# Four blocks of a feed-forward product as a two-by-two scheme of seven products, with its operands kept in HBM

## The chip, the cores and the metric

The kernel runs on one core of one Trainium2 chip. The metric is the device time of one execution in microseconds (us), as the median of several runs. A core has five engines that run beside each other: TensorE (PE; its weight loads are listed as PEld), VectorE (DVE), ScalarE (ACT), GpSimd (POOL) and SyncE (SP), on whose queue this kernel issues all of its DMAs.

## The reference

One decoder layer on 1024 tokens of width 1024: a half-step feed-forward part, a token mixer with two groups of heads, and a second feed-forward part, each followed by a layer norm.

```
x = LN1(ALPHA * x + 0.5 * swiglu(x, w_gate1, w_up1, w_down1))
x = LN2(ALPHA * x + mixer(x))
x = LN3(ALPHA * x + 0.5 * swiglu(x, w_gate2, w_up2, w_down2))
swiglu(x, g, u, d) = (silu(x @ g) * (x @ u)) @ d        # D_FF = 2816
```

All of it is in float32. Only the two swiglu parts matter here.

## The kernel before

**Tiles.** The 2816 hidden channels are 22 blocks of 128. Tokens are two halves of 512. For a block and a half, the hidden value silu(gate) * up is a tile of 128 channels by 512 tokens; w_down is applied with a chunk of 128 tokens of it as the stationary operand and a block of w_down, 128 channels by 512 output columns (again two halves), as the moving one. The results are added on DVE into `acc`, eight tiles of 128 tokens by 1024 columns (`down`, L213 to L235).

**Precision.** Each float32 operand is split into a high part (a cast on ACT, L135) and a low part (a subtraction on DVE, L136), and a product is three matmuls: high by high, high by low, low by high.

**Blocks in pairs.** Blocks 2 to 11 of the first feed-forward part and blocks 8 to 17 of the second are worked in pairs by `ffn_pairs` (L580). Gate and up of a pair are a two-by-two block product done with seven products instead of eight (`PRODUCTS`, `weight_sums` L472, `project` L505): each product P1 to P7 is 12 matmuls (four pieces of the sums of tokens by three). The sums of tokens are made once (`token_sums` L452, `last_sums` L462); the sums of weight halves are made for each pair on DVE from four loads (t11, t21, t12, t22) and a fifth tile t2. Products with one target accumulate in one PSUM bank; two banks serve the gate (tag pa) and two others the up product (tag pm). `keep` copies an intermediate value out of the bank on ACT, and `done` finishes one of four hidden tiles, "11" to "22" (token half, block of the pair). There, for the up product, the hidden tile is split at once into its parts gh and gl (L534 to L536).

**w_down of a pair** is done without such a scheme: `down_turns` makes 16 tiles (2 column halves x 2 token halves x 4 chunks), each of 2 blocks x 3 matmuls, in the steps marked d of TURNS, between the products of the next pair; the last pair's 16 steps come at the end. `halves_of` loads and splits the w_down blocks.

**Order and look-ahead.** A turn is one product (12 matmuls) or one d step (6 matmuls). The list `need` holds the weight operands in the order of their use, and the loop at L616 makes them up to DEEP = 4 ahead of the turn. A scheduler then sets the order on each engine by a model of the times, near to the written order but not equal to it; on SP a DMA that waits holds up those behind it.

**Buffers.** Raw loads go to a ring of 7 tiles with the tag wr, split weights to 6 pairs wh and wl, split hidden values to 4 pairs gh and gl, hidden values to 4 tiles gs and kept products to 3 tiles sn. A PSUM bank is 128 x 512 float32; there are 2 with the tag pa, 3 with pd and 3 with pm.

**Around it.** `run` (L1074) begins with blocks 0 and 1 of the first part for both halves, without the scheme for seven products (`hidden_first` L363, `hidden` L351). In this stretch acc holds raw x; `load_acc` loads x into acc again afterwards, beside the first turns, where the token sums are made too.

Of the kernel before, what the change touches and what calls it, by code (L numbers as in the profile page):

```python
# [10 lines left out]
F32 = mybir.dt.float32  # L11
# [37 lines left out]
TURNS = "ggddddgddddgddddgddddgguuuuuuu"  # L49
DEEP = 4  # L50
# [36 lines left out]
class Layer:  # L87
    def __init__(self, tc, ctx, a):
# [13 lines left out]
        self.sx, self.kept = {}, {}  # L102
# [241 lines left out]
    def up(self, w, half, s, pool, tags, bufs):  # L344
        ps = yield from self.proj(w, half)
        self.nc.vector.tensor_tensor(s[:], s[:], ps[:], ALU.mult)
        hs = [self.wt(pool, [HT], t, bufs, F32R) for t in tags]
        self.split(hs[0][:], hs[1][:], s[:])
        return hs
# [155 lines left out]
    def project(self, ops, hid, up):  # L505
# [9 lines left out]
        def done(n, w):  # L515
# [45 lines left out]
    def down_turns(self, ops, hid):  # L561

        for d in range(2):
            for i in range(2):
                for c in range(4):
                    yield
                    hs = [hid[f"{i + 1}1"], hid[f"{i + 1}2"]]
                    ws = [{d: ops[n, d]} for n in range(2)]
                    now(self.down(hs, ws, i, 0.5, [c], cuts=((d * HT, (d + 1) * HT),)))

    def halves_of(self, blocks):
        for d in range(2):
            for b in blocks:
                raw = self.u("wr", self.wp)
                self.nc.sync.dma_start(raw[:], b[:, HALVES[d]])
                hl = [self.wt(self.wp, [HT], "w" + e, BUFS["w"], F32R) for e in "hl"]
                self.split(hl[0][:], hl[1][:], raw[:])
                yield hl

    def ffn_pairs(self, idx, fs, before=None, beside={}):  # L580

        gu, wd = self.a[f"gu{idx}"], self.a[f"wd{idx}"]
        order = [n for n, b in PRODUCTS]
        turns, need = [], []

        def plan(f, before, kinds):

            hid, work, asks = {}, {}, {}  # L590
            if before:
                keys = [(n, d) for d in range(2) for n in range(2)]
                asks["d"] = [keys[:2]] + [[]] * 7 + [keys[2:]] + [[]] * 7
                work["d"] = {}, before[1], self.halves_of([wd[before[0] + n] for n in range(2)])
            if f is not None:
                for up in range(2):

                    blocks = [m[:, sl] for sl in HALVES for m in (gu[f, up], gu[f + 1, up])]
                    asks["gu"[up]] = [[n] for n in order]
                    work["gu"[up]] = {}, hid, self.weight_sums(order[4:], *blocks)  # L600
            makes = {k: self.down_turns(w[0], w[1]) if k == "d" else self.project(w[0], w[1], k == "u") for k, w in work.items()}
            for make in makes.values():
                next(make)
            for kind in kinds:
                if kind in work:
                    ops, _, weights = work[kind]
                    for n in asks[kind].pop(0):
                        need.append((ops, n, weights))
                    turns.append((makes[kind], len(need)))
            return f, hid  # L610

        for f in range(fs.start, fs.stop, 2):
            before = plan(f, before, TURNS)
        plan(None, before, "d" * 16)
        made = 0
        for t, (make, asked) in enumerate(turns):  # L616
            while made < min(asked + DEEP, len(need)):
                ops, n, weights = need[made]
                ops[n] = next(weights)
                made += 1  # L620
            for work in beside.get(t, ()):
                work()
            next(make, None)

# [449 lines left out]
    def run(self):  # L1074
# [5 lines left out]
        with self.phase("fs") as self.fs, self.phase("fa") as self.fx:  # L1080
            self.scr = "gs", self.fx
            hs = [self.hidden_first(self.fx, ("gh", "gl"), 4)]
            hs.append(now(self.hidden(1, 1, (0, 1), self.fx, ("gh", "gl"), 4)))
            hid = {f"{i + 1}{j + 1}": hs[j][i] for i in range(2) for j in range(2)}
            beside = {t: [lambda q=t: self.token_sums(q)] for t in range(KB // 2)}
            for t in range(4):
                beside[t] += [lambda c=c: self.load_acc(c, 0) for c in (2 * t, 2 * t + 1)]
                beside[6 + t] = [lambda c=c: self.load_acc(c, 1) for c in (2 * t, 2 * t + 1)]
                beside[6 + t].append(lambda q=t: self.last_sums(q))
            self.ffn_pairs(1, range(2, K1), (0, hid), beside)  # L1090
# [7 lines left out]
        with self.phase("fs") as self.fs, self.phase("fb") as self.fx:  # L1098
# [4 lines left out]
            self.ffn_pairs(2, range(K2, NF - LAST), beside={t: [lambda q=t: self.last_sums(q)] for t in range(KB // 2)})  # L1103
# [115 lines left out]
```

## Time and profile before

| | |
|---|---|
| time, median of 3 runs | 2053.87 us (2052.97 to 2054.53) |
| time of the profiled execution | 2053.73 us |
| its span, first to last instruction | 2051.8 us |
| mean granted clock of TensorE | 0.997 |
| PE busy | 2020.1 us, 98%, 10052 instructions |
| DVE busy | 1370.5 us, 67%, 2925 instructions |
| ACT busy | 849.3 us, 41%, 1685 instructions |
| DMA | 251.19 MB, mean 122 GB/s |

The profile is of one execution. A group's row names the line, the engine, the operation and its tiles, the count, the time busy and the mean duration in nanoseconds, and the idle time of the engine before these instructions with what ended it. A row of a stretch gives, for each engine, the busy time in that stretch and the number of instructions that began in it. Matmuls are pipelined, so a matmul's drawn duration is longer than the distance between the starts of two; neighbours on DVE overlap a little too. Some matmul records can be missing, a few per cent at most.

### The profile page before, as it was taken

What the parts mean: (1) busy time and instruction counts of PE and PEld (TensorE: products, weight loads), DVE (VectorE), ACT (ScalarE), POOL (GpSimd) and SP (SyncE); (2) the same over time, 40 slices, a digit from 0 to 9 for tenths busy, and PEclk for the clock granted to TensorE, in tenths of its full rate; (3) what the DMA queues carried; (4) which work ended last, traced back from release to release, by engine and by line L of the source; (5) the groups of instructions that cost most, each with busy time, mean ns of one, the idle gap of its engine ahead of it and who ended that gap; (6) DMA issues with size and microseconds to landing.
All of it is one profiled execution on the core that took longest, in us unless ns stands there. A gap on an engine that the chain in (4) does not pass through costs nothing.

```text
span 2051.8 us, 28207 instructions
## 1 busy us (share of the span) xinstructions
PE 2020.1 (98%) x10052; PEld 1650.5 (80%) x10052; DVE 1370.5 (67%) x2925; ACT 849.3 (41%) x1685; POOL 50.2 (2%) x87
## 2 busy tenths in 40 slices
PE   9999999999999999999999999999999999999998
PEld 7788888888888777788788777788788888888887
DVE  5865566545668787746887687667856766556566
ACT  4423333232554444445466545454433423333332
POOL 0000000000000000000100000000000000000000
PEclk9999999999999999999999999999999999999999
DMA  4711112565554344435354434333443311112331
GB/s 172 248 46 58 52 62 86 180 197 188 172 195 143 125 144 144 142 119 182 124 193 132 133 108 123 95 103 114 139 138 119 113 57 47 62 52 88 122 118 63
DMA packets 136653, 251.19 MB, mean 122 GB/s; under 512 B 15552, under 2 KB 16064, under 8 KB 136512
## 3 DMA queue, kind: packets, MB, share of 16 engines
q1 hardware_dynamic: 136512, 249.39, 37.7%
q8 instruction: 79, 1.29, 0.3%
q14 instruction: 62, 0.51, 0.1%
HBM read 206.34 MB, written 42.99 MB: 122 GB/s over the span
## 4 chain that ended last, share of the span: by engine, by line
PE 85%; DVE 8%; ACT 2%; DMA 2%; issue 1%; POOL 0%; SPq 0%; DVEq 0%; ACTq 0%; POOLq 0%
PE pa L207 10%; PE pa L208 10%; PE pa L210 10%; PE pd L229 9%; PE pd L231 9%; PE pd L230 8%; PE pm L547 3%; PE pm L548 3%; PE pm L549 3%; PE pa L547 3%; PE pa L548 3%; PE pa L549 3%; PE pm L1041 1%; DVE wl L136 1%; PE pm L640 1%
## 5 line engine op out<-in xcount | busy, mean ns | idle before, releaser
L135 ACT CAST wh<-wr 128x512 fp32r<-128x512 f32 (+1 forms) x461 | 285.7, 621 | 701.6 <-PE pa L208 207.7
L207 PE MATMUL pa<-xh,wh 128*128 128x512 f32 x1168 | 469.7, 402 | 9.2 <-ACT xh L135 4.6
L136 DVE TENSOR_TENSOR wl<-wr,wh 128x512 fp32r<-128x512 f32 (+1 forms) x461 | 314.6, 686 | 229.5 <-ACT wh L135 226.5
L208 PE MATMUL pa<-xl,wh 128*128 128x512 f32 x1168 | 461.6, 395 | 0.1
L210 PE MATMUL pa<-xh,wl 128*128 128x512 f32 x1152 | 454.3, 395 | 0.0
L234 DVE SCALAR_TENSOR_TENSOR acc<-pd,acc 128x512 f32<-128x512 f32 x433 | 292.9, 685 | 97.3 <-PE pd L231 94.9
L207 PEld LDWEIGHTS pa<-xh,wh 128*128 128x128 f32 x1168 | 220.7, 189 | 56.1 <-ACT xh L135 5.7
L208 PEld LDWEIGHTS pa<-xl,wh 128*128 128x128 f32 x1168 | 220.7, 189 | 42.8 <-DVE xl L136 2.1
L210 PEld LDWEIGHTS pa<-xh,wl 128*128 128x128 f32 x1152 | 217.3, 189 | 43.1
L229 PE MATMUL pd<-wh,gh 128*128 128x512 f32 (+1 forms) x450 | 175.0, 390 | 0.5 <-DVE acc L234 0.4
L231 PE MATMUL pd<-wh,gl 128*128 128x512 f32 (+1 forms) x450 | 174.8, 389 | 0.0
L230 PE MATMUL pd<-wl,gh 128*128 128x512 f32 (+1 forms) x450 | 174.8, 388 | 0.0
L229 PE MATMUL pd<-wh,hh 128*128 128x512 f32 x352 | 141.6, 406 | 1.5 <-ACT xf L278 1.5
L230 PE MATMUL pd<-wl,hh 128*128 128x512 f32 x352 | 139.9, 398 | 1.0 <-DVE wl L136 1.0
L231 PE MATMUL pd<-wh,hl 128*128 128x512 f32 x352 | 139.4, 398 | 0.0
L149 ACT CAST wh<-wr 128x512 fp32r<-128x512 f32 x132 | 80.0, 620 | 84.4 <-PE pa L208 63.6
L229 PEld LDWEIGHTS pd<-wh,gh 128*128 128x128 f32 x450 | 84.5, 188 | 20.0 <-ACT gh L135 1.6
L231 PEld LDWEIGHTS pd<-wh,gl 128*128 128x128 f32 x450 | 84.5, 188 | 18.4 <-DVE gl L136 1.1
L150 ACT CAST wl<-wr 128x512 fp32r<-128x512 f32 x132 | 81.1, 618 | 41.5 <-PE pd L230 39.1
L230 PEld LDWEIGHTS pd<-wl,gh 128*128 128x128 f32 x450 | 84.5, 188 | 16.9
L229 PEld LDWEIGHTS pd<-wh,hh 128*128 128x128 f32 x352 | 66.6, 189 | 19.7 <-ACT hh L135 4.1
L231 PEld LDWEIGHTS pd<-wh,hl 128*128 128x128 f32 x352 | 66.4, 189 | 15.0 <-DVE hl L136 2.5
(454 smaller groups left out, 3179.5 us busy)
## 6 DMA issues: line engine op xcount, KB each, us to landing
wr<-gu SPq DMA_DIRECT2D x263, 256.0 KB, 2.9
wr<-wd SPq DMA_DIRECT2D x132, 256.0 KB, 2.7
kept<-wl SPq DMA_DIRECT2D x132, 256.0 KB, 2.2
wr<-kept SPq DMA_DIRECT2D x132, 256.0 KB, 2.8
wr<-win SPq DMA_DIRECT2D x116, 256.0 KB, 3.1
wr<-wout SPq DMA_DIRECT2D x32, 256.0 KB, 3.0
wr<-xT SPq DMA_DIRECT2D x28, 256.0 KB, 3.0
wr<-x2d SPq DMA_DIRECT2D x28, 256.0 KB, 2.7
```

The source lines that it names most:

```text
L135: self.nc.scalar.copy(hi, src)
L136: self.nc.vector.tensor_tensor(lo, src, hi.bitcast(F32), ALU.subtract)
L207: nc.tensor.matmul(ps[:], hi[:, sl], xh[k][:], start=(k == 0), stop=False)
L208: nc.tensor.matmul(ps[:], hi[:, sl], xl[k][:], start=False, stop=(lo is None and k == KB - 1))
L210: nc.tensor.matmul(ps[:], lo[:, sl], xh[k][:], start=False, stop=(k == KB - 1))
L229: nc.tensor.matmul(p, hh[:, sl], wh[:, ds], start=(i == 0), stop=False)
L230: nc.tensor.matmul(p, hh[:, sl], wl[:, ds], start=False, stop=False)
L231: nc.tensor.matmul(p, hl[:, sl], wh[:, ds], start=False, stop=(i == n - 1))
L234: nc.vector.scalar_tensor_tensor(acc, p, scale / ALPHA, acc, ALU.mult, ALU.add, accum_out=None if sums is None else sums[:, d:d + 1])
L547: nc.tensor.matmul(ps[:], op[0][:, sl], xh[:], start=new, stop=False, skip_group_check=True)
L548: nc.tensor.matmul(ps[:], op[0][:, sl], xl[:], start=False, stop=False, skip_group_check=True)
L549: nc.tensor.matmul(ps[:], op[1][:, sl], xh[:], start=False, stop=q == 3, skip_group_check=True)
```

## The change

Both feed-forward parts now do the w_down products of two groups of four blocks by the scheme of seven products: blocks 0 to 3 and 4 to 7 in the first part, 8 to 11 and 12 to 15 in the second. The two-by-two blocks are token halves by pairs of blocks, and pairs of blocks by column halves. A product is 4 chunks x 2 blocks x 3 matmuls; P1, P6, P7 and P4 go on accumulating in the same bank (three banks pd and one pm, held for the whole group), and P2, P5 and P3 take a bank pm each time. The pairs that remain, blocks 8 to 11 and 16 to 17, keep w_down without the scheme (`down_two`), one token half used for both column halves in a row.

The hidden values are no longer split where they are made. They are written to HBM as float32 (`put`, two turns after they are made at the earliest), and so are their sums, which `first_pair` and `second_pair` make on DVE; the second pair reads two values of the first back to make them. Each product's operands are then loaded from HBM and split right before use (`hidden_parts`). The sums of w_down blocks are made in `four_operands`, two of them being written to HBM and read again.

STEPS gives the number of w_down steps that lie between the 14 products of each pair (0 for the first pair of the first part and the first two of the second); what is left, 24 steps in each part, follows the last pair. The up product uses the two pa banks too. DEEP is 5. The token sums of the first part are made while block 1 is worked, the last sums beside the first turns, and acc is loaded beside turns 3 to 10.

```diff
-TURNS = "ggddddgddddgddddgddddgguuuuuuu"
-DEEP = 4
+DOWN = (("P1", ((0, 0),)), ("P2", ((0, 0),)), ("P6", ((0, 1),)), ("P5", ((0, 1), (1, 1))), ("P3", ((0, 1),)),
+        ("P7", ((1, 1),)), ("P4", ((1, 0),)))
+
+STEPS = {1: (0, 14, 14, 18, 18), 2: (0, 0, 14, 14, 20)}
+DEEP = 5
...
@@ project
-            hl = [self.wt(self.fx, [HT], "g" + e, 4, F32R) for e in "hl"]
-            self.split(hl[0][:], hl[1][:], g[:])
-            hid[n] = hl
+            hidden(n, g)
...
+            if up:
+                hidden(n)
             if not banks:
-                banks.extend(self.bank("pm" if up else "pa") for _ in range(2))
+                banks.extend(self.bank("pa") for _ in range(2))
...
+    def put(self, key, t):
+        def work():
+            self.hbm[key] = self.dp.tile([P, HT], F32, name=self.nm("hid"), tag="hid" + "_".join(map(str, key)), bufs=1)
+            self.nc.sync.dma_start(self.hbm[key][:], t[:])
+        self.later.append((self.turn + 2, work))
...
+    def first_pair(self, g):
...
+            i, q = int(n[0]) - 1, int(n[1]) - 1
+            got[i, q] = t
+            self.put((g, ("P1", "A21")[i], q), t)
+            if (1 - i, q) in got:
+                s3 = self.u("sn", self.fx)
+                self.nc.vector.tensor_tensor(s3[:], got[0, q][:], got[1, q][:], ALU.subtract)
+                self.put((g, "P7", q), s3)
...
+    def second_pair(self, g):
...
+            if t is None:
+                q = {"P7": 1, "P4": 0}.get(n)
+                if q is not None:
+                    parts[q] = [self.load(self.hbm[g, a, q][:]) for a in ("A21", "P1")]
+                return
+            i, q = int(n[0]) - 1, int(n[1]) - 1
+            got[i, q] = t
+            self.put((g, ("P2", "P4")[i], q), t)
+            if i:
+                s1, s2 = parts[q]
+                tt(s1[:], s1[:], t[:], ALU.add)
+                tt(s2[:], s1[:], s2[:], ALU.subtract)
+                self.put((g, "P5", q), s1)
+                self.put((g, "P6", q), s2)
+                sums[q] = s2
+            if (1 - i, q) in got:
+                s4 = self.u("sn", self.fx)
+                tt(s4[:], got[0, q][:], sums[q][:], ALU.subtract)
+                self.put((g, "P3", q), s4)
...
+    def hidden_parts(self, *key):
+        return self.parts(self.load(self.hbm[key][:]), self.fx, "g", 4)
...
+    def four_operands(self, g, blocks):
+        b = lambda j, d, q: self.load(blocks[2 * j + q][:, HALVES[d]])
...
+        for n, _ in DOWN:
+            for q in range(2):
+                yield self.hidden_parts(g, n, q)
+            for q in range(2):
+                if n == "P1":
+                    t = b(0, 0, q)
+                elif n == "P2":
+                    t = b(1, 0, q)
+                elif n == "P6":
+                    t1, b11, t = b(0, 1, q), b(0, 0, q), b(1, 1, q)
+                    tt(t1[:], t1[:], b11[:], ALU.subtract)
+                    self.put((g, "T1", q), t1)
+                    tt(t[:], t[:], t1[:], ALU.subtract)
+                    self.put((g, "T2", q), t)
+                elif n == "P5":
+                    t = self.load(self.hbm[g, "T1", q][:])
+                elif n == "P3":
+                    t = b(1, 1, q)
+                elif n == "P7":
+                    t, b12 = b(1, 1, q), b(0, 1, q)
+                    tt(t[:], t[:], b12[:], ALU.subtract)
+                else:
+                    t, t2 = b(1, 0, q), self.load(self.hbm[g, "T2", q][:])
+                    tt(t[:], t[:], t2[:], ALU.subtract)
+                yield self.down_parts(t)
+
+    def down_four(self, ops):
...
+        for n, outs in DOWN:
+            for c in range(4):
+                yield
+                if n == "P1":
+                    sums.append(self.bank("pm" if c == 3 else "pd"))
+                chained = n in ("P1", "P6", "P7", "P4")
+                ps = sums[c] if chained else self.bank("pm")
...
+                for q in range(2):
+                    (hh, hl), (wh, wl) = ops[n, "h", q], ops[n, "w", q]
...
+                for i, d in outs:
+                    acc = self.acc[4 * i + c][:, HALVES[d]]
+                    nc.vector.scalar_tensor_tensor(acc, ps[:], 0.5 / ALPHA, acc, ALU.mult, ALU.add)
+
+    TWO = ((0, 1), (0, 0), (1, 0), (1, 1))
...
@@ ffn_pairs
+        fours = [start + 4 * j for j in range(2)]
+        queue = [(idx, f, 4) for f in fours] + [(idx, f, 2) for f in range(start + 8, fs.stop, 2)]
...
+            for t, w in enumerate(work):
+                turn(*w)
+                while done < count * (t + 1) // len(work):
+                    turn(*step())
+                    done += 1
+        while steps or queue:
+            turn(*step())
...
@@ run
-            hs = [self.hidden_first(self.fx, ("gh", "gl"), 4)]
-            hs.append(now(self.hidden(1, 1, (0, 1), self.fx, ("gh", "gl"), 4)))
...
+            hs = [self.hidden_first(None, None, 0)]
...
+                if n % 7 == 2 and sums:
+                    self.token_sums(sums.pop(0))
...
+            beside = {t: [lambda q=t: self.last_sums(q)] for t in range(KB // 2)}
+            for t in range(8):
+                beside.setdefault(t + 3, []).extend(lambda d=d, c=t: self.load_acc(c, d) for d in range(2))
```

More of the change, by code (lines that the diff above doesn't have):

```diff
@@ L101, in __init__ @@
         self.centred = {}
[L102 removed]
+        self.sx, self.kept, self.hbm = {}, {}, {}
+        self.later, self.turn = [], 0
         self.x2d = {}
@@ L580, in ffn_pairs, with put_now @@
-    def ffn_pairs(self, idx, fs, before=None, beside={}):
-        gu, wd = self.a[f"gu{idx}"], self.a[f"wd{idx}"]
+    def put(self, key, t):
[3 more added lines that the diff above has]
+        self.later.append((self.turn + 2, work))
+    def put_now(self):
+        while self.later and self.later[0][0] <= self.turn:
+            self.later.pop(0)[1]()
@@ new lines, in lone_pair, with parts, down_parts @@
+    def lone_pair(self, g):
+        return lambda n, t=None: None if t is None else self.put((g, int(n[0]) - 1, int(n[1]) - 1), t)
+    def parts(self, t, pool, tag, bufs):
+        hl = [self.wt(pool, [HT], tag + e, bufs, F32R) for e in "hl"]
+        self.split(hl[0][:], hl[1][:], t[:])
+        return hl
+    def hidden_parts(self, *key):
+        return self.parts(self.load(self.hbm[key][:]), self.fx, "g", 4)
+    def down_parts(self, t):
+        return self.parts(t, self.wp, "w", BUFS["w"])
@@ new lines, with two_operands, down_two @@
+    TWO = ((0, 1), (0, 0), (1, 0), (1, 1))
+    def two_operands(self, g, blocks):
+        for n, (d, i) in enumerate(self.TWO):
+            if n != 2:
+                for q in range(2):
+                    yield self.hidden_parts(g, i, q)
+            if n % 2 == 0:
+                for q in range(2):
+                    yield self.down_parts(self.load(blocks[q][:, HALVES[d]]))
+    def down_two(self, ops):
+        hs, ws = None, None
+        for n, (d, i) in enumerate(self.TWO):
+            for c in range(4):
+                yield
+                if c == 0 and n != 2:
+                    hs = [ops[n, "h", q] for q in range(2)]
+                if c == 0 and n % 2 == 0:
+                    ws = [{d: ops[n, "w", q]} for q in range(2)]
+                now(self.down(hs, ws, i, 0.5, [c], cuts=((d * HT, (d + 1) * HT),)))
@@ L585, in ffn_pairs @@
+    def ffn_pairs(self, idx, fs, first=0, beside={}):
+        gu = self.a[f"gu{idx}"]
         order = [n for n, b in PRODUCTS]
         turns, need = [], []
[L588 to L602, printed above, removed]
-                next(make)
[L604 to L610, printed above, removed]
@@ L612, in ffn_pairs, with step @@
-        for f in range(fs.start, fs.stop, 2):
-            before = plan(f, before, TURNS)
-        plan(None, before, "d" * 16)
+        start = fs.start - first
+        fours = [start + 4 * j for j in range(2)]
+        queue = [(idx, f, 4) for f in fours] + [(idx, f, 2) for f in range(start + 8, fs.stop, 2)]
+        steps = []
+        def step():
+            if not steps:
+                idx, f, n = queue.pop(0)
+                ops, asks, make, weights = self.down_steps(idx, (idx, f), f, n)
+                next(make)
+                steps.extend((ops, ask, make, weights, (idx, f), n) for ask in asks)
+            return steps.pop(0)
@@ new lines, in turn @@
+        def turn(ops, asks, make, weights, g=None, blocks=0):
+            for n in asks:
+                key = None
+                if g and n[1] == "h":
+                    key = g, n[0] if blocks == 4 else self.TWO[n[0]][1], n[2]
+                need.append((ops, n, weights, key))
+            turns.append((make, len(need)))
+        for f, count in zip(range(fs.start, fs.stop, 2), STEPS[idx]):
+            g = (idx, max([h for h in fours if h <= f < h + 4], default=f))
+            take = self.lone_pair(g) if g[1] not in fours else self.first_pair(g) if g[1] == f else self.second_pair(g)
+            hid = {}
+            work = []
+            for up in range(2):
+                blocks = [m[:, sl] for sl in HALVES for m in (gu[f, up], gu[f + 1, up])]
+                ops = {}
+                make = self.project(ops, hid, up, take)
+                next(make)
+                weights = self.weight_sums(order[4:], *blocks)
+                work += [(ops, [n], make, weights) for n in order]
+            done = 0
+            for t, w in enumerate(work):
[3 more added lines that the diff above has]
+                    done += 1
```

83 lines of the change are left out of this document (57 added, 26 removed).

## The prediction

> **What bounds the kernel now.** I read the page's head and engine row first, then the chain that ended last, then stretches of the span, then PE, DVE and SP in order of time.
>
> ```profile
> span 2051.8 us, 28207 instructions
> PE 2020.1 (98%) x10052; PEld 1650.5 (80%) x10052; DVE 1370.5 (67%) x2925; ACT 849.3 (41%) x1685; POOL 50.2 (2%) x87
> PE 85%; DVE 8%; ACT 2%; DMA 2%; issue 1%; POOL 0%; SPq 0%; DVEq 0%; ACTq 0%; POOLq 0%
> ```
>
> PE is busy for 98% of the span and carries 85% of the chain; the question is whether a matmul less is time less in the stage where it goes. The stretches (PE, PEld, DVE, ACT, POOL busy with their instructions, granted clock, DMA share, GB/s) answer that for the stage with the pairs (100:350 here, 1600 to 1910 in the second FFN) and give neighbours with more load:
>
> ```profile
> 30.00:40.00 10.00, 10.00 (x46) 8.29 (x45) 4.33 (x8) 2.46 (x4) 0.00 (x0) 1.00 0.00 1
> 40.00:50.00 10.00, 10.00 (x46) 8.29 (x45) 4.30 (x7) 2.66 (x5) 0.00 (x0) 1.00 0.26 79
> 50.00:100.00 50.00, 48.50 (x210) 38.38 (x209) 42.27 (x69) 21.73 (x38) 0.00 (x0) 1.00 0.75 254
> 100.00:350.00 250.00, 250.00 (x1100) 205.87 (x1099) 150.08 (x232) 80.03 (x138) 0.31 (x1) 1.00 0.17 55
> 350.00:550.00 200.00, 200.00 (x878) 163.61 (x877) 112.98 (x184) 63.21 (x106) 4.25 (x12) 1.00 0.59 191
> 600.00:800.00 200.00, 198.05 (x1146) 160.63 (x1145) 157.08 (x438) 96.14 (x234) 9.09 (x18) 1.00 0.42 138
> 1000.00:1050.00 50.00, 44.57 (x222) 35.11 (x221) 45.02 (x102) 31.45 (x59) 4.30 (x6) 0.97 0.53 174
> 1600.00:1650.00 50.00, 49.97 (x218) 40.28 (x217) 36.04 (x58) 20.64 (x35) 0.00 (x0) 1.00 0.30 95
> ```
>
> In 100:350 PE is never idle, DVE is busy for 150 of 250 us and the DMA engines for 17%. Busy PE could still be PE waiting inside a matmul, so the pitch is read from starts in order of time:
>
> ```profile
> 301.51 0.39 PE L229 MATMUL pd<-wh,gh 128*128 128x512 f32 x1
> ...
> 306.95 0.39 PE L547 MATMUL pa<-P60h,wh 128*128 128x512 f32 x1
> 109.89 0.39 PE L549 MATMUL pm<-xh,wl 128*128 128x512 f32 x1
> 110.11 0.39 PE L547 MATMUL pm<-P30h,wh 128*128 128x512 f32 x1
> ...
> 110.80 0.39 PE L547 MATMUL pm<-P31h,wh 128*128 128x512 f32 x1
> 111.13 0.50 PE L547 MATMUL pm<-xh,wh 128*128 128x512 f32 x1
> ...
> 115.57 0.39 PE L549 MATMUL pm<-P33h,wl 128*128 128x512 f32 x1
> ```
>
> Between the first two rows lie 24 matmuls of w_down: 5.44 us, 0.2267 us each, though each is drawn 0.39 long. That pitch is the price of a matmul, and no idle time beside it could swallow the saving.
>
> **The change part by part.** *Matmuls removed.* Four blocks against w_down take 16 tiles of 4 blocks of 3 matmuls, 192; seven products take 7 x 4 chunks x 2 blocks x 3 = 168. Four groups lose 96 matmuls on the bounding engine: 96 x 0.2267 = 21.8 us. The Trainium skill (TensorE: Matmul & The Clock Gate, Back-to-back issue gap) gives about 131 ns for a sustained N = 512 matmul with its weight load; by that the saving would be 12.6 us and the sum 2045, an estimate. The trace has 227 ns, and that row decides.
>
> *DVE and ACT added.* The rows for one operation, and four neighbours on DVE:
>
> ```profile
> L136 DVE TENSOR_TENSOR wl<-wr,wh 128x512 fp32r<-128x512 f32 x459 | 313.8, 687 | 226.5 <-ACT wh L135 223.5 <-DMA wr<-gu 2.0 <-PE pa L210 0.5
> L135 ACT CAST wh<-wr 128x512 fp32r<-128x512 f32 x459 | 284.9, 622 | 700.9 <-PE pa L208 207.7 <-PE pd L231 198.0 <-PE pa L548 146.9
> 222.38 0.69 DVE L532 TENSOR_TENSOR sn<-sn,pm 128x512 f32<-128x512 f32 x1 [1.35 <-PE pm L549]
> 222.99 0.68 DVE L136 TENSOR_TENSOR wl<-wr,wh 128x512 fp32r<-128x512 f32 x1
> 223.59 0.69 DVE L533 TENSOR_TENSOR gs<-gs,sn 128x512 f32<-128x512 f32 x1
> 224.19 0.69 DVE L491 TENSOR_TENSOR wr<-wr,wr 128x512 f32<-128x512 f32 x1
> ```
>
> Two pairs cost DVE today 2 x (22 for weight sums and low parts + 14 behind the projections + 20 for w_down) = 112 operations. Afterwards: 2 x (22 + 10), 2 + 6 sums of hidden values, 28 low parts, 8 weight sums and 32 accumulations = 140. So 28 more per group, 28 x 0.687 = 19.2 us; ACT has 12 more casts, 7.5 us. Neither is on the path if it fits. The fullest pair is one with 14 steps of w_down: (168 + 84) x 0.2267 = 57.1 us of PE, and 70 DVE operations: 48.1 us as drawn, 84%. But neighbours start 0.603 us apart (222.38 to 224.19 is three), so DVE needs 42.2 us, 74%. ACT has 40 operations, some 25 us. Both fit on average; the cover is the operands made ahead. If DVE falls behind by more than about two products (8 us), PE waits for low parts.
>
> What such density costs is bounded by rows. Loaded are the pairs with steps and the tails: four pairs of 14 steps (57.1 us), two of 18 (62.6), one of 20 (65.3), two tails of 24 x 6 matmuls (32.6), 484 us. Lower bound: none, as in 100:350. Upper bound: 50:100, DVE 85% drawn, where 210 matmuls stand instead of 221, 5%: 24 us. The nearest row is 600:800: DVE 157 of 200 us (79%), PE idle 1.95 us, 1%. I take that: +4.7 us.
>
> *HBM added.* Per group 32 loads (14 hidden, 14 more of w_down, 4 for the sums) and 20 writes of 256 KB:
>
> ```profile
> q1 hardware_dynamic: 136512, 249.39, 37.7%
> wr<-gu SPq DMA_DIRECT2D x263, 256.0 KB, 2.9
> wr<-wd SPq DMA_DIRECT2D x132, 256.0 KB, 2.7
> kept<-wl SPq DMA_DIRECT2D x132, 256.0 KB, 2.2
> wr<-kept SPq DMA_DIRECT2D x132, 256.0 KB, 2.8
> ```
>
> The first pair of a group with 14 steps moves 8 + 20 loads and 10 writes, 10 MB in 57.1 us, 174 GB/s. In 350:550 the same queue moves 191 GB/s, of the same size and both ways, and PE loses nothing; so bandwidth costs nothing. A load that reads back what was written waits on SP for the write, and everything queued on SP behind it waits too: the other loads and the writes. The closest such couple is T1, written for product P6 and read for P5, four steps or 4 x 18 x 0.2267 = 16 us later, against 2.2 us to land; a hidden value is read a pair later. Zero; without that distance it would be 2.2 us each.
>
> *The ring of seven wr tiles.* This is the resource that gets tight. SP's own waits in 100:350:
>
> ```profile
> SPq L478 <- DVE wl L136: 125.1, 28, 14.8
> SPq L575 <- DVE wl L136: 90.4, 18, 14.8
> ```
>
> SP waits for a free tile for 216 of 250 us: all seven are always held, today for prefetch. A pair of 60 us takes 14 tiles, so each is held 7 x 60 / 14 = 30 us. After the change a group's second pair takes 34: ten for weight sums, 20 for w_down, four for the values read back. What they need at least: a step of 18 matmuls is 4.08 us; the five tiles of a weight sum serve 3, 5, 3, 5 and 3 products, 77 us, with loads and splitting 96, twice 191; eight hidden and four w_down tiles of 2.9 + 1.3 us, 50; P7 and P4, 33; four sums of 14 us (load, wait for the product, two sums, two turns, write), 56. That is 330 of 7 x 57.1 = 400 us, 2 us of slack for each tile. A first pair needs some 300 with 30 tiles, 3.4 us. It fits without a long prefetch. Taken at zero; the rival below prices the other end.
>
> *The start.* In 50:100, 11 matmuls (2.5 us) are missing while the token sums are made, with the DMA engines at 75%. The change makes them during block 1, where (30:50) DVE is busy 43% and DMA at most 26%. Between nothing and 2.5 us gained; half, -1.2. What moves on SP there: the 16 loads of the token sums come earlier, the 8 of the last sums too, six writes join, and the 16 loads of acc go behind them; acc is first added to when the second pair's steps begin, 38 us (168 x 0.2267) later, so nobody waits for them. In return blocks 0 and 1 split nothing there, four casts and four DVE operations fewer.
>
> *Pairs without steps* (one in the first FFN, two in the second) leave nothing to put between P7 and P4, which share a bank. Today's up products have no cover either: P7 ends at 109.89, P3's first matmuls are put between, and P4 starts 0.33 after 110.80 instead of 0.227, 0.1 us. Six projections at 0.1: +0.6; at most, if P4 waited for a whole addition and its ends, 1 us each, 6. That up now shares gate's two banks costs nothing for the same reason: P3 lies between the last reader and the next writer.
>
> *Nothing:* PSUM tiles are evicted 32 times per group in both; the longer tail (24 steps for 16) is PE work in any case and its last operands have 8 steps, 11 us, for write, load and split (2.2 + 2.9 + 1.3).
>
> **Sum.** The profiled execution took 2053.73 us (1.9 outside the span). 2053.7 - 21.8 + 4.7 - 1.2 + 0.6 = 2036.0. The median of the runs is 0.14 above that execution: 2036. What is late next is PE again.
>
> **The rivals.** *DVE is late often (no difference).* If the loaded 484 us run as 50:100 does, 24 us come back: 2053.7 - 21.8 + 24 = 2056. For it: drawn 84% there and 85% here. Against it: 50:100 also has DMA at 75%, and 1600:1650 with DVE at 72% lost three matmuls at most.
>
> *The ring binds (slower).* If tiles are held longer than needed, SP cannot load in time, since it issues in order and a load without a tile stops those behind it. Each microsecond beyond the slack costs 34 / 7 = 4.9 us in a second pair, 30 / 7 = 4.3 in a first. Held 5 us over the minimum: 2 x 3.0 x 4.9 + 2 x 1.6 x 4.3 = 43 us, so 2053.7 - 21.8 + 43 = 2075. It decides from 3.9 us (2 x 1.9 x 4.9 + 2 x 0.5 x 4.3 = 23, the whole gain). For it: P6 needs three tiles per block with two writes before they come free, and the values read back come just then for the next pair's loads. Against it: the loads land within 2.9 us and there is 17 to 25% of slack. The granted clock would show it too: in 1000:1050, with 5.4 us of PE idle, it fell to 0.97, 1.5 us more. The Trainium skill (TensorE: Matmul & The Clock Gate, on HAM oscillation) has the clock halved after an idle gap of some 3.4 us until PE has been busy as long; the trace agrees in kind, and by that each such stall would cost 1.7 us more, an estimate.
>
> **How the numbers follow.** The forecast has 0.70 (its own range 2030 to 2048: no stall and the whole gain at the start, to 2% of stalls with the whole price of the uncovered projections), DVE late 0.14, the ring 0.16. A difference of 0.2%, about what can be told from none, is 4.1 us: faster means below 2049.8. A third of the DVE rival reaches below that. Faster 0.74, same 0.10, slower 0.16. The range goes from 2029, a little below the forecast's best, to 2060, past the DVE rival; most of the ring rival stays out.
>
> **What would show it.** Right: 9956 PE instructions, stretches in the loaded pairs with 218 to 221 matmuls per 50 us, DVE near 84% drawn there, queue q1 near 312 MB, and no long PE wait on a low part of w. Wrong: PE waits in the loaded pairs of over 1%, behind low parts whose idle time before them ends with a DMA into wr (the ring), or with DVE itself never idle (DVE). The forecast falls if the loaded pairs' pitch is above 0.238 us per matmul (5%).

## The result and the profile after

The changed kernel takes 2029.65 us in the median of 4 runs (2026.02 to 2030.21), the kernel before 2054.2 in 4 on the same chip: a ratio of their means of 0.9876, with a 95% interval of 0.9859 to 0.9893. It is faster, by 24.5 us between the medians where 18 were forecast. The profiled execution took 2030.06 us against 2053.73, its span 2028.3 against 2051.8: 23.5 us less. The head of the page after, its engine row and its DMA queue:

```profile
span 2028.3 us, 28810 instructions
PE 1995.8 (98%) x9956; PEld 1632.1 (80%) x9956; DVE 1435.8 (71%) x3043; ACT 875.2 (43%) x1739; POOL 50.3 (2%) x87
PE 84%; DVE 8%; DMA 3%; ACT 3%; issue 2%; POOL 1%; SPq 0%; DVEq 0%; ACTq 0%; POOLq 0%
q1 hardware_dynamic: 170784, 311.80, 48.1%
```

96 matmuls fewer and 62 MB more on the queue are as worked out. DVE has 118 operations more and ACT 54, six more each than the prediction's 28 and 12 per group make (112 and 48): in the three pairs that keep the plain form two hidden values are now split twice. PE bounds as before. The stretches of the kernel after that answer to those shown of before (PE, PEld, DVE, ACT, POOL, granted clock, DMA share, GB/s):

```profile
0.00:50.00 50.00, 44.38 (x179) 35.27 (x180) 39.39 (x63) 29.00 (x48) 0.34 (x5) 1.00 0.82 269
50.00:100.00 50.00, 50.00 (x220) 40.72 (x219) 33.48 (x52) 19.66 (x34) 0.00 (x0) 1.00 0.80 265
...
100.00:330.00 230.00, 229.47 (x1013) 189.72 (x1012) 171.84 (x273) 85.51 (x152) 1.55 (x7) 1.00 0.51 161
...
1700.00:1850.00 150.00, 150.00 (x664) 124.24 (x663) 117.59 (x188) 56.19 (x99) 0.00 (x0) 1.00 0.56 182
1850.00:1890.00 40.00, 39.09 (x172) 31.71 (x171) 32.65 (x54) 13.87 (x24) 0.00 (x0) 1.00 0.62 193
```

The first steps of w_down are at 94.4 and 1678.3 us, so the last three rows hold most of the loaded pairs and the second tail. PE is idle there for 0.5 of 230 us, nothing in 150 and 0.9 in 40. The 220 matmuls in 50:100 were 210 before.

What PE itself waited for in both pair stages (50:400, then 1590:1910) is three waits in all. A row gives the total in us, the number of waits and the longest:

```profile
PE pa L554 <- DVE gs L530: 0.5, 1, 0.5
PE pd L234 <- DVE acc L239: 0.4, 1, 0.4
```

```profile
PE pd L234 <- DVE acc L239: 0.8, 1, 0.8
```

Each is for a PSUM bank that DVE has still to read: the first for the bank that P7 leaves and P4 takes, the others for banks of w_down at the end of the stage. None is for an operand.

Where the 23.5 us come from is read off four points of the traces: the first product of the pairs in each part, the last w_down matmul of the first part's pairs, and the end. First the kernel before, the matmuls of its product line in two windows and the last w_down matmul in order of time:

```profile
L547 PE MATMUL pa<-xh,wh x16: 389/389/499, 52.8 to 94.5; 128*128 128x512 f32 x16
```

```profile
378.59 0.39 PE L231 MATMUL pd<-wh,gl 128*128 128x512 f32 x1
```

```profile
L547 PE MATMUL pa<-xh,wh x32: 389/389/498, 1605.4 to 1688.3; 128*128 128x512 f32 x32
```

Then the same of the kernel after (`53.0 to 97.8` in a row are the first and the last start within the window):

```profile
L554 PE MATMUL pa<-xh,wh x40: 389/389/501, 53.0 to 97.8; 128*128 128x512 f32 x40
```

```profile
365.46 0.39 PE L236 MATMUL pd<-wh,gl 128*128 128x512 f32 x1
```

```profile
L554 PE MATMUL pa<-xh,wh x80: 389/389/504, 1591.5 to 1698.3; 128*128 128x512 f32 x80
```

| stretch | before | after | difference | 48 matmuls fewer make |
|---|---|---|---|---|
| start to the pairs | 52.8 | 53.0 | +0.2 | |
| pairs of the first part, to the last w_down | 325.8 | 312.5 | -13.3 | -10.9 |
| from there to the pairs of the second part | 1226.8 | 1226.0 | -0.8 | |
| from there to the end | 446.4 | 436.8 | -9.6 | -10.9 |

Of the first part's extra 2.4 us, 2.3 are the ten matmuls more in 50:100 (10 x 0.2267). So by this account its loaded pairs cost nothing beyond their matmuls, and those of the second part 1.3 us.

### The profile page after: what moved, and what is told of

The parts are those of the page before. It is cut to its first block, busy times and chain, and to the rows that moved or that the text cites. A ratio compares the mean times of both kernels' runs of the same rounds, so it can differ in the third digit from the quotient of the medians.

```text
span 2028.3 us, 28810 instructions
## 1 busy us (share of the span) xinstructions
PE 1995.8 (98%) x9956; PEld 1632.1 (80%) x9956; DVE 1435.8 (71%) x3043; ACT 875.2 (43%) x1739; POOL 50.3 (2%) x87
## 4 chain that ended last, share of the span: by engine, by line
PE 84%; DVE 8%; DMA 3%; ACT 3%; issue 2%; POOL 1%; SPq 0%; DVEq 0%; ACTq 0%; POOLq 0%
PE pa L212 11%; PE pa L213 11%; PE pa L215 11%; PE pa L554 6%; PE pa L555 6%; PE pa L556 6%; PE pd L234 5%; PE pd L236 5%; PE pd L235 5%; PE pm L689 1%; PE pm L688 1%; PE pm L690 1%; PE pm L1211 1%; DVE acc L239 1%; PE pm L810 1%
## 5 line engine op out<-in xcount | busy, mean ns | idle before, releaser
L140 ACT CAST wh<-wr 128x512 fp32r<-128x512 f32 (+1 forms) x485 | 298.3, 620 | 645.6 <-PE pa L213 201.6
L212 PE MATMUL pa<-xh,wh 128*128 128x512 f32 x1168 | 469.9, 402 | 9.3 <-ACT xh L140 5.6
L141 DVE TENSOR_TENSOR wl<-wr,wh 128x512 fp32r<-128x512 f32 (+1 forms) x485 | 329.5, 686 | 203.6 <-ACT wh L140 199.1
L213 PE MATMUL pa<-xl,wh 128*128 128x512 f32 x1168 | 461.4, 395 | 0.1
L215 PE MATMUL pa<-xh,wl 128*128 128x512 f32 x1152 | 454.1, 394 | 0.0
L239 DVE SCALAR_TENSOR_TENSOR acc<-pd,acc 128x512 f32<-128x512 f32 x305 | 205.3, 685 | 50.5 <-PE pd L236 48.9
L554 PE MATMUL pa<-xh,wh 128*128 128x512 f32 x320 | 125.5, 392 | 0.5 <-DVE gs L530 0.5
L555 PE MATMUL pa<-xl,wh 128*128 128x512 f32 x320 | 124.6, 389 | 0.0
L556 PE MATMUL pa<-xh,wl 128*128 128x512 f32 x320 | 124.6, 389 | 0.0
L234 PE MATMUL pd<-wh,gh 128*128 128x512 f32 (+1 forms) x194 | 75.8, 393 | 1.4 <-DVE acc L239 1.2
L235 PEld LDWEIGHTS pd<-wl,hh 128*128 128x128 f32 x352 | 66.4, 189 | 12.6 <-DVE wl L141 1.4
L236 PE MATMUL pd<-wh,gl 128*128 128x512 f32 (+1 forms) x194 | 75.1, 388 | 0.0
```

The source lines that it names most:

```text
L140: self.nc.scalar.copy(hi, src)
L141: self.nc.vector.tensor_tensor(lo, src, hi.bitcast(F32), ALU.subtract)
L212: nc.tensor.matmul(ps[:], hi[:, sl], xh[k][:], start=(k == 0), stop=False)
L213: nc.tensor.matmul(ps[:], hi[:, sl], xl[k][:], start=False, stop=(lo is None and k == KB - 1))
L215: nc.tensor.matmul(ps[:], lo[:, sl], xh[k][:], start=False, stop=(k == KB - 1))
L234: nc.tensor.matmul(p, hh[:, sl], wh[:, ds], start=(i == 0), stop=False)
```

## The experiments

Theory 1, formed from these rows: the 96 matmuls at their pitch and the start are the gain, and the added work is hidden because the operands are made far enough ahead. Rivals: other parts of the change gain by themselves; the dense stretch costs what the prediction charged and something else pays for it; the ring of seven tiles takes a part. Ratios below are to runs of the kernel before that were taken alongside, with their intervals. Costs and gains against the changed kernel are differences of two such ratios, and by their intervals each is uncertain by 4 to 5 us.

**The groups undone.** All groups as pairs in the plain form, the rest as changed. With the 96 matmuls this also takes away what the seven products need: their sums and the extra loads and writes.

```diff
-        fours = [start + 4 * j for j in range(2)]
+        fours = []
-STEPS = {1: (0, 14, 14, 18, 18), 2: (0, 0, 14, 14, 20)}
+STEPS = {1: (0, 18, 18, 18, 18), 2: (0, 0, 18, 18, 20)}
-            take = self.first_pair((1, 0))
+            take = self.lone_pair((1, 0))
```

> This kernel is the changed one with all w_down products in the plain form, pair by pair: the hidden values still pass through HBM, the up products still use the two pa banks, the start is the new one; only the four groups with seven products, and with them the 96 matmuls, are undone. Theory 1 (the matmuls are the whole gain but for the start): PE gets its 96 matmuls back at 0.2267 us, 21.8 us, so 2029.7 + 21.8 = 2051.5, between 2050 and 2053.5, which is the kernel before less about 2.2 us of the start. Rival (the new order, the look-ahead of 5 or the shared banks gain time by themselves): below 2048. Rival (the passage through HBM costs time that the seven products had to pay first): above 2056.

Measured: 2049.83 us, ratio 0.9985 (0.9976 to 0.9993). That is 0.0109 above the changed kernel's 0.9876, 22.4 us, for 21.8 expected. It is the net of the matmuls saved and the work added: had that work cost 4.7 us, 17 would stand here. What remains without the seven products is a gain of 3 us (1.4 to 4.9), of which the start explains 2; the rest isn't told apart from none. The passage through HBM costs nothing that can be seen, here at 99 GB/s in 100:350. PE's waits in the first pair stage are of the same kind as in the changed kernel, 0.6 us for DVE L530 and 0.8 for L239, though DVE is busy for only 61% of 100:330; in the second stage there is none. So in the first stage even these small waits come without the added work.

**The start alone.** In the kernel before, the token sums are made while block 1 is worked; nothing else is changed.

```diff
-            hs.append(now(self.hidden(1, 1, (0, 1), self.fx, ("gh", "gl"), 4)))
+            work = self.hidden(1, 1, (0, 1), self.fx, ("gh", "gl"), 4)
...
+                if n % 7 == 2 and sums:
+                    self.token_sums(sums.pop(0))
```

> This is the kernel before with one part of the change: the token sums of the first feed-forward part are made while block 1 is worked. Theory 1: the 2.5 us of gaps between 50 and 100 us go, all but some 0.4, so the time falls by 2.1 us, to 2052.1, and the stretch 50:100 has 219 to 221 matmuls. The prediction's term: half of it, 1.2 us. Rival: the start's gain in the changed kernel comes from the w_down steps and the loads of acc having left that stretch, not from the sums; then nothing changes here, 2054.2 and 210 to 213 matmuls.

Measured: 2051.47 us, ratio 0.9992 (0.9983 to 1.0001), 1.6 us, not told apart from none by time alone. The stretches of this kernel say more:

```profile
0.00:50.00 50.00, 44.80 (x174) 35.01 (x175) 38.51 (x62) 30.04 (x50) 0.34 (x5) 1.00 0.81 275
50.00:100.00 50.00, 50.00 (x222) 41.14 (x221) 30.83 (x48) 16.32 (x28) 0.00 (x0) 1.00 0.49 157
```

50:100 is dense, with 222 matmuls for 210; 0:50 has 174 for 180. So the sums' place is the cause of the gaps, the rival falls, and the net is six matmuls, 1.4 us. It is the prediction's size (1.2); in the changed kernel the two stretches together have nine more, 2.0 us.

**More work for DVE, unpinned.** One or three additions of zeros behind each product of the loaded pairs (they add nothing to the result).

```diff
             next(make, None)
             self.turn += 1
+            if t in loaded:
+                for _ in range(1):          # 3 in the other run
+                    self.nc.vector.tensor_tensor(j[:], z[:], z[:], ALU.add)
```

> The changed kernel with one more DVE addition of 128x512 (zeros into a tile that nothing uses but a last write) behind each of the 14 products of the seven loaded pairs, 98 in all. In a pair of 14 steps DVE then has 84 operations for 57.1 us of PE: 57.7 us as drawn (101%), 50.7 us by the distance of neighbours of 0.603 us (89%). Theory 1 (DVE's capacity goes by the distance, and what is below it is covered by the operands made ahead): at most 2 us more, 2029.7 to 2031.7, PE still without long waits. Rival (the prediction's density rule: PE loses 1% at a drawn share of 79% and 5% at 85%): at least 5% of some 420 us, 20 us, 2050 or more.

> The same with three such additions per product, 294 in all. A pair of 14 steps has 112 DVE operations, 67.5 us by the distance, 10.4 us more than PE needs. Theory 1 (by the distance): the four pairs of 14 steps lose 10.4 us each, the others 5 to 10 each, some 65 us together, less what is put off into the tail: 2029.7 + 45 to 70, 2075 to 2100. By drawn durations (0.687 us, 77 us) it would be 20 us for each pair of 14 steps and some 130 us together, 2160. Density rule: no number beyond at least 20 us.

Measured: 2037.24 us, ratio 0.992 (0.9907 to 0.9934), and 2052.01, 1.0003 (0.9994 to 1.0012): 9 and 26 us over the changed kernel. The first lies outside both theories; the second is below theory 1's 45 to 70 and meets the density rule's "at least 20". The trace shows why neither number tests them. Nothing ties these additions to a time, and the scheduler put them as early as DVE had room. In the run with one per product, the group of these additions in 0:100 is

```profile
L801 DVE TENSOR_TENSOR zz<-zz 128x512 f32<-128x512 f32 x42 | 28.8, 686 | 1.9 <-POOL zz L738 1.3
```

42 of the 98, where no loaded pair is in work yet, and PE lost its time there, as the stretch shows (190 matmuls for 220):

```profile
50.00:100.00 50.00, 45.77 (x190) 36.10 (x189) 45.45 (x74) 17.43 (x31) 0.00 (x0) 0.97 0.71 238
```

The run with three still tells something, by its stretches:

```profile
100.00:150.00 50.00, 49.41 (x219) 40.59 (x218) 48.62 (x80) 20.42 (x36) 0.00 (x0) 1.00 0.58 183
150.00:200.00 50.00, 49.57 (x219) 40.74 (x218) 48.41 (x80) 20.23 (x37) 0.00 (x0) 1.00 0.49 155
200.00:250.00 50.00, 50.00 (x223) 41.40 (x222) 49.70 (x83) 15.64 (x28) 0.00 (x0) 1.00 0.62 198
250.00:300.00 50.00, 42.91 (x172) 32.79 (x170) 49.50 (x83) 13.85 (x24) 0.00 (x0) 0.94 0.35 111
```

DVE is busy for 97 to 99% and PE has 219 to 223 matmuls in three stretches, then breaks. A busy share alone doesn't slow PE; it matters what the busy engine puts off.

**More work for DVE, pinned.** The additions now read the product's high weight part, so that they fall where that part is made and used.

```diff
+            for _ in range(more):           # 1 or 2 in a loaded pair
+                tt(self.zj[1][:], op[0][:].bitcast(F32), self.zj[0][:], ALU.add)
```

> The changed kernel with one more DVE addition behind each of the 14 products of the seven loaded pairs, 98 in all, that reads the product's high weight part, so that it can't run before that part is made and a later weight part can't take the tile before it is done (in the two earlier runs with additions the scheduler put most of them into the start). DVE in a pair of 14 steps: 84 operations, 50.7 us by the distance of neighbours of 57.1 us, 89%. Theory 1 (what is below DVE's capacity is covered): at most 3 us more, 2029.7 to 2032.7. Rival (density): PE loses 5% or more of the loaded 420 us, 2050.

> The same with two such additions per product, 196 in all: 98 operations in a pair of 14 steps, 59.1 us by the distance, 2.0 us more than PE's 57.1; the pair of 20 steps is even, those of 18 within 1.3. Theory 1: four pairs lose 2 us each and the queue's delays at the edge of capacity add as much again: 8 to 20 us, 2038 to 2050. By drawn durations (67.3 us for 57.1) the four pairs alone would lose 41 us and the three others some 9 each: 2098.

Measured: 2035.5 us, ratio 0.9915 (0.9902 to 0.9928), 8 us more than the changed kernel (its profiled span 4.3 more); and 2048.74, 0.9982 (0.9973 to 0.9991), 22 us more. The stretches with one:

```profile
100.00:150.00 50.00, 50.00 (x221) 41.22 (x220) 43.35 (x70) 19.37 (x34) 0.00 (x0) 1.00 0.52 169
150.00:200.00 50.00, 50.00 (x222) 41.33 (x222) 46.50 (x77) 19.83 (x35) 0.00 (x0) 1.00 0.50 162
200.00:250.00 50.00, 47.37 (x203) 38.78 (x202) 42.81 (x70) 17.81 (x31) 0.00 (x0) 0.97 0.61 198
250.00:300.00 50.00, 50.00 (x221) 41.03 (x220) 43.35 (x72) 19.76 (x35) 0.00 (x0) 1.00 0.46 153
```

DVE is busy for 86 to 93%, and PE is dense but for one break of some 18 matmuls (203 for 221), 4 us. PE at that break, and DVE just before it:

```profile
230.18 0.76 PE L554 MATMUL pa<-xh,wh 128*128 128x512 f32 x1 [2.63 <-DVE gs L530]
```

```profile
228.74 0.69 DVE L659 TENSOR_TENSOR wr<-wr,wr 128x512 f32<-128x512 f32 x1 [0.94 <-DMA wr<-wd]
229.35 0.68 DVE L530 TENSOR_TENSOR gs<-sn,pa 128x512 f32<-128x512 f32 x1
```

P4 waits for DVE to read P7's bank. That read stands on DVE behind a sum of w_down blocks for P6 (L659), and DVE itself is idle for 0.94 us until the load for that sum lands. So this break isn't an engine that is full: a load that came late reached PE through the order of work on DVE. The additions also keep each split weight tile until they have read it; whether this or DVE's delay made the load late wasn't taken apart. With two:

```profile
100.00:150.00 50.00, 49.76 (x220) 40.90 (x219) 49.17 (x81) 19.61 (x33) 0.00 (x0) 1.00 0.50 162
...
200.00:250.00 50.00, 49.02 (x213) 39.13 (x212) 49.58 (x83) 17.75 (x31) 0.00 (x0) 1.00 0.61 201
250.00:300.00 50.00, 45.62 (x191) 36.34 (x190) 46.31 (x77) 16.93 (x30) 0.00 (x0) 0.97 0.45 147
```

Here DVE is full (98, 99 and 93%), and PE falls back to 213 and 191. With one addition theory 1 expected at most 3 us and the density rule 20; neither holds. With two, theory 1's 8 to 20 us (2038 to 2050) came near. DVE's capacity does go by the distance of neighbours (by drawn durations the run with two would have lost 68 us), but the last tenth of it wasn't free in these runs: about 1 us at the change's own 75 to 82%, then 8 us more at 86 to 93% and 22 us more when DVE is full. As the break shows, these aren't prices of DVE's share alone.

**The ring, first try.** One or two wr tiles were to be held through the pair stages.

```diff
+        held = [self.u("wr", self.wp) for _ in range(2)]      # 1 in the other run
+        for h in held:
+            self.nc.gpsimd.memset(h[:, 0:16], 0.0)
...
+        for h in held:                                        # behind the last turn
+            self.nc.gpsimd.memset(h[:, 0:16], 0.0)
```

> The changed kernel with one of the seven wr tiles held by two small writes from the first to the last turn of both pair stages, so that six serve the loads there. The prediction's floor for a second pair with steps was 330 of the ring's time, here 6 x 57.1 = 343. Theory 1 (loads need little more than that floor): 0 to 3 us more, 2029.7 to 2033. Rival (tiles are held some microseconds over the floor, and the ring is nearly the bound at seven): 9 us or more for each second pair with steps and 4 for the other loaded pairs, some 40 us, 2070.

> The same with two tiles held, so that five serve the loads, as many as one weight sum holds at once. Theory 1 (the floors are right): a second pair needs (330 - 286) / 5 = 9 us more, a first or lone pair (300 - 286) / 5 = 3 us, together 2 x 9 + 5 x 3 = 33 us, so 2063, between 2050 and 2085, and the PE waits in the loaded pairs end with casts whose own waits end with a DMA. If time stays below 2040, the floors were too high and the ring is no limit anywhere near.

Measured: 2029.47 us, 0.9888 (0.9874 to 0.9902), and 2029.83, 0.9889 (0.9876 to 0.9903). These look like a ring with room to spare, and are not. POOL in order of time in the run with two:

```profile
36.80 0.11 POOL L781 MEMSET wr<- 128x16 f32 x1 [35.94 <-DVE P52l L141]
36.97 0.11 POOL L798 MEMSET wr<- 128x16 f32 x1
37.14 0.11 POOL L781 MEMSET wr<- 128x16 f32 x1
37.31 0.11 POOL L798 MEMSET wr<- 128x16 f32 x1
```

The closing writes (L798) follow the first ones at once, since POOL had nothing else to wait for; no tile was held. The runs say nothing on the ring.

**The ring, held.** The closing write now reads acc after its last accumulation.

```diff
-            self.nc.gpsimd.memset(h[:, 0:16], 0.0)
+            self.nc.vector.tensor_copy(h[:, 0:16], self.acc[KB - 1][:, D - 16:D])
```

> The changed kernel with one of the seven wr tiles really held in both pair stages: it is written before the first turn and last written by DVE from acc after the last accumulation, so that it can't come free between. (In the two ring runs before this one both writes fell together at the start of the stage, and nothing was held.) Theory 1 (loads need little more than the prediction's floor of 330 of the ring's time, here 343): 0 to 3 us more, 2029.7 to 2033. Rival (seven tiles are nearly the bound): 9 us or more for each second pair with steps and 4 for the other loaded pairs, some 40 us, 2070.

Measured: 2051.22 us, ratio 0.9992 (0.9982 to 1.0002), 24 us more than the changed kernel. Theory 1's 3 us fall, and the rival's 40 are too many; but its claim, that seven tiles lie near the edge, is what the run shows. By the prediction's floor, 330 of ring time for 343, six would have been enough. Two held tiles weren't run. Stretches of the run with six, then of the kernel after:

```profile
94.00:330.00 236.00, 228.60 (x977) 185.73 (x976) 173.51 (x275) 86.38 (x153) 0.00 (x0) 0.98 0.50 164
```

```profile
94.00:330.00 236.00, 235.47 (x1039) 194.71 (x1038) 176.84 (x282) 88.26 (x156) 1.55 (x7) 1.00 0.52 164
```

62 matmuls fewer in the same time, 14 us, with DVE and DMA no busier; in 1700:1850 it is 633 for 664, 7 us more. What ACT waited for there, in the run with six and in the kernel after:

```profile
ACT wh L140 <- DMA wr<-wd: 24.5, 6, 10.1
...
ACT wh L140 <- PE pa L555: 19.8, 8, 4.3
```

```profile
ACT wh L140 <- PE pa L555: 61.6, 25, 4.3
...
ACT wh L140 <- DMA wr<-wd: 9.2, 3, 4.2
```

With seven tiles ACT's casts mostly wait for PE to free a split tile: they are ahead. With six they wait more for loads, and PE's longest waits in this stretch (2.6 and 2.1 us) are for such casts.

**Ten tiles.** Does the ring take something at seven that other gains hide?

```diff
-BUFS = {... "wr": 7, ...}
+BUFS = {... "wr": 10, ...}
```

> The changed kernel with ten wr tiles instead of seven, in all of the kernel. With one tile fewer it lost 24 us, so seven lie at the edge. Theory 1 (at seven the ring just covers; what is left in the loaded pairs is about 1 us): 0 to 2.5 us less than the changed kernel's ratio of 0.9876, within 0.986 to 0.989, and the loaded stretches with 221 or 222 matmuls. Rival (the ring still takes a visible part at seven, which the other gains hide): 5 us or more less, below 0.9855.

Measured: 2027.65 us, ratio 0.987 (0.9852 to 0.9888); the profiled span is 2025.8 us. Against the changed kernel's 0.9876 that is 1.2 us with intervals that overlap, no proven gain; in 94:330 it has 1038 matmuls and in 1700:1850 662, the changed kernel 1039 and 664. So at seven the ring covers, and the small cost of the loaded pairs doesn't hide a cost of the ring.

**A shorter look-ahead.**

```diff
-DEEP = 5
+DEEP = 3
```

> The changed kernel with a look-ahead of 3 operands instead of 5. Theory 1 (the cover of the dense stretch is the operands made ahead): less cover, PE waits appear in the loaded pairs, most at P6 where a w operand takes three loads; 3 to 15 us more, 2033 to 2045. Rival (the order is set by the scheduler and by free tiles, and the written look-ahead hardly matters): within 2 us of 2029.7.

Measured: 2033.49 us, ratio 0.9906 (0.9892 to 0.9919), 6 us more, inside theory 1's 3 to 15 and outside the rival's 2. So the look-ahead matters. That the operands came late isn't shown: of the 4.4 us that PE waits in the two pair stages of this trace, 4.0 are for PSUM banks that ACT or DVE had still to read, and 0.4 for an operand.

**A third group.** Blocks 8 to 11 of the first part as a group as well, with its 28 steps at the end; then with 4 of them moved between the products; then the first of these with ten tiles.

```diff
-        fours = [start + 4 * j for j in range(2)]
+        fours = [start + 4 * j for j in range((fs.stop - start) // 4)]
-STEPS = {1: (0, 14, 14, 18, 18), ...
+STEPS = {1: (0, 14, 14, 14, 14), ...     # (0, 16, 16, 14, 14) in the second
```

> The changed kernel with blocks 8 to 11 of the first feed-forward part as a third group of four there, all of its 28 steps behind the last pair (14 steps between the products of each of the four pairs before). 24 matmuls fewer, 5.4 us. Theory 1: the tail has 28 steps, 38.1 us of PE, beside some 68 DVE operations, 41 us by the distance, so some 3 us come back, 0 to 4: 2029.7 - 5.4 + 3 = 2027, between 2024 and 2029.7. Rival (the late values of the second pair must be written, read back and split before P6 and stall PE): 2033 or more.

> The changed kernel with a third group in the first feed-forward part (blocks 8 to 11), as in the run before with three groups, but with 16, 16, 14 and 14 steps between the products, so that the third group's P1 is done before the last pair ends and 24 steps are left instead of 28. 24 matmuls fewer than the changed kernel, 5.4 us. In the run with 28 steps in the tail PE lost some 11 us there against the changed kernel. Theory 1 (the tail was DVE's and the DMA queue's, by its length): half of that loss goes, 2029.7 - 5.4 + 5 = 2029, between 2026 and 2033. Rival (the loss is the chain of write, load and split of the late values, whatever the length): 2035 again.

> The kernel with three groups in the first feed-forward part and 28 steps behind its last pair, with ten wr tiles. At seven its tail (320:370) lost some 28 matmuls, 7 us, and gave up its 5.4 us. Theory 1 (in that tail the ring keeps SP from loading ahead, with the DMA engines at 88% and DVE at 89%, so that more tiles give part of it back): 3 to 6 us less than with seven, 0.989 to 0.990. Rival (the tail is bound by the DMA engines and DVE themselves, or by the chain of write, load and split): within 2 us of 0.9921.

Measured: 2035.5 us, 0.9921 (0.9907 to 0.9935); 2046.67, 0.9972 (0.9963 to 0.9981); and 2036.37, 0.9914 (0.9898 to 0.9931). All are slower than the changed kernel though they have 24 matmuls less. The first and the third came out as their rivals had it; the second is outside both of its theories (2026 to 2033, and 2035). The tail of the first, and the longest wait of PE in the second (starts in order of time):

```profile
320.00:370.00 50.00, 42.85 (x172) 32.08 (x170) 44.35 (x73) 20.50 (x35) 0.10 (x1) 0.97 0.83 272
```

```profile
338.63 0.80 PE L688 MATMUL pm<-wh,gh 128*128 128x512 f32 x1 [7.84 <-ACT wh L140]
```

Where the changed kernel has 218 matmuls in 320:370, this one has 172, with DVE at 89% and the DMA engines at 83%. Ten tiles change nothing, so it isn't the ring. With the shorter tail it is slower still: PE stands for 7.84 us on a cast. SP's queue in order of time just before, in that run:

```profile
332.14 0.33 SPq L572 DMA_DIRECT2D hid<-sn  x1
332.52 0.45 SPq L186 DMA_DIRECT2D small<-small  x1
333.02 0.45 SPq L187 DMA_DIRECT2D rowb<-row  x1
333.59 0.36 SPq L456 DMA_DIRECT2D wr<-hid  x1
```

The loads of hidden values begin only behind the last write of the pair's values and some constants of the next stage, 5 us ahead of the matmul that waits. Whether that order, or DVE and the DMA engines together, is the cause wasn't taken apart.

## Why the prediction was too cautious

Point by point:

- *Matmuls removed, 21.8 us:* right. 22.4 us between the changed kernel and the plain one, and each part of the trace is shorter by about the 10.9 us of its 48 matmuls. The pitch of 0.227 us holds. By the 131 ns that the Trainium skill gives (TensorE: Matmul & The Clock Gate, Back-to-back issue gap) the two kernels would lie 12.6 us apart; page and measurement differ, and the measurement decides.
- *The start, -1.2:* right in kind, short by a little. 1.4 us with the sums alone, 2.0 in the changed kernel.
- *Pairs without steps, +0.6:* nothing visible; 50:100, where such a pair lies, is dense.
- *HBM and SP, zero:* right. 161 and 182 GB/s in the loaded stretches with PE dense, and 20 more writes and 32 more loads per group at no cost.
- *The ring, zero at seven:* right, ten tiles gained nothing that can be told from none. The floor of 330 behind it was too low to size a ring, though: at six, 343 of ring time, it still fitted, and 24 us were lost. The need lies between 343 and the 400 of seven tiles. That the ring binds when it is short, as the rival had it, is real; its condition wasn't met.
- *The density of the loaded pairs, +4.7 us:* this is the step that failed. It measured some 1 us (nothing in the first part, 1.3 in the second). The prediction took PE's 1% idle time in 600:800 of the kernel before as the price of a DVE busy for 79%, and looked at that share alone. What PE waited for in that stretch, and the two longest rows of its weight loads, are in the kernel before:

```profile
PE pa L207 <- ACT q L714: 0.6, 1, 0.6
PE pm L640 <- DVE mi L844: 0.4, 1, 0.4
PE pm L1041 <- DVE vb L1035: 0.4, 1, 0.4
```

```profile
PEld pm L913 <- ACT mi L911: 2.8, 8, 0.4
PEld pm L894 <- ACT mi L890: 1.5, 4, 0.4
```

All of these are waits of the token mixer, for its own values and banks. L890 to L913, for instance, are its solve and its state update, where a matmul's operand is the result of the one before it, a copy away. The pairs have no such chain. That the same share of DVE does not bring the same loss is shown within the changed kernel: with DVE at 80% PE is idle for 1.65 of 200 us in its 600:800, and with DVE at 78% for nothing in 150 us in its 1700:1850. That the mixer's waits would be there with an idle DVE as well is an argument from the program; no run took DVE's load away there.

There was a second fault in the same step. The 84% was right as a sum of drawn durations (in 1700:1850, 188 operations of 0.686 us make 129 of 150 us, 86%), but it was set beside the shares of stretches, in which an overlap counts once; there the row has 117.6 us. In that measure the loaded pairs stand at 75 to 82%, about the share of 600:800, and PE lost nothing in most of it. Above that share the pinned additions did cost time, 8 and 22 us.

The path was another one, too. The prediction had a late DVE reach PE through low parts of w. Where PE waited, it was for a PSUM bank that DVE had still to read, three times and 1.7 us in all, and the plain form has such waits as well.

- *Elsewhere:* 0.8 us less between the two pair stages, where nothing was meant to change, has no cause here; it is within what runs of one kernel differ by (2026.0 to 2030.2 for the changed one).

The mechanism of the likeliest case, fewer matmuls at their pitch with the rest hidden, was right; it carried a cost borrowed from a stage with other waits, and without that cost its sum would have been 2031. The remaining 1 to 2 us are the start, the pairs without steps and the stretch between the stages, none of which can be told from none by time alone.

## What to carry to other kernels

Where one engine never waits, the price of an instruction taken from it is its pitch times the count, and work added to other engines is nearly free as long as operands stay ahead and banks are read in time: check the pitch by neighbours, and the cover by what the feeding engines wait for (PE means ahead, DMA means behind). A neighbouring stretch gives a price only if its waits have the same releasers; read those before borrowing its idle share. When a buffer ring is budgeted, the least time for which each tile must be held is only a floor: here a ring 4% over it lost 24 us, and one 21% over it lost nothing that shows.

## What the runs showed of the hardware that was not expected

DVE at 97 to 99% and PE at 219 to 223 matmuls per 50 us went together for 150 us (100:250 of the run with three additions). And one ring tile of 256 KB less cost 24 us, about as much as the 96 matmuls had brought.
